# Scale and shift of the first layer by fp32 weights held in TensorE, with five row blocks of sixteen on VectorE

## The chip, the cores and the metric

The kernel is one program on one core of a Trainium2 chip. The metric is the device time of one execution in microseconds (us), the median over the runs. A profile of one execution lists every instruction of the engines: TensorE (PE for its matmuls, PEld for its loads of the stationary operand), VectorE (DVE), ScalarE (ACT), GpSimd (POOL) and SyncE (SP), on whose queue the loads from memory are issued.

## What is computed

Two layers of a backbone with four parallel branches work on 256 latent and 256 context tokens of 2048 features. The change is in the first step of the first layer, the adaptive normalisation (adaLN):

```python
shift, scale, gate = jnp.split(jax.nn.silu(c) @ w_ada[l] + b_ada[l], 3, axis=-1)
shift_c, scale_c, gate_c = jnp.split(jax.nn.silu(c_ctx) @ w_ada[l] + b_ada[l], 3, axis=-1)
h = modulate(x, g_pre[l], shift[:, None], scale[:, None])      # rms_norm(x, g) * (1 + scale) + shift
hc = modulate(ctx, g_pre[l], shift_c, scale_c)
p = split_proj(h @ w_in[l])
```

So two vectors, silu(c) for the latents (stream 0) and silu(c_ctx) for the context (stream 1), are multiplied by a matrix of 2048 rows; 4096 of its columns, shift and scale, are needed before the first projection can take its input. The normalisation needs the sum of squares of each token over the 2048 features. All is fp32.

## The kernel before

Features lie on the partitions, tokens along the free dimension: `x[k]`, k = 0 to 15, is 128 features by 512 tokens (both streams). A matmul of the projections splits each operand into a rounded part (`h`, made by ScalarE's cast) and the rest (`l`, made by VectorE's subtraction), both of type fp32r, and adds three products (`mm3`, L165 to L167 in the profile): hh x wh, hl x wh, hh x wl.

`startup` makes shift and scale in eight groups. Group g covers features of `x[2g]` and `x[2g+1]`: 512 columns, pieces of 128 for scale and shift of the two tiles. A group's weights are 2048 rows, that is 16 row blocks (`rb`) of 128 rows by 512 columns. They come in four units (q = 0 to 3) of 1 MB; a unit has two halves, a half two row blocks (the index i). The loads are issued in the order of the units, three buffers (`NRAW`) ahead. For each block ScalarE casts (L279) and VectorE subtracts (L286), and TensorE holds four columns of `sc4` (the two parts of the two vectors) and streams the block through, once for each part (L439, L440):

```python
w = self.sc4[:, 4 * rb:4 * rb + 4]
T.matmul(pa[g][0:4, :], w, hi[i], start=rb == 0, stop=False)
T.matmul(pa[g][0:4, :], w, lo[i], start=False, stop=rb == 15)
```

The result is four rows in the PSUM bank `pa`. ScalarE copies them (L446), four transposes bring them onto partitions (L451), VectorE adds the parts (L459, L461) and makes the factors `ab` (L410, L412), multiplies the two tiles of x by the tokens' reciprocal roots R (L454), and `build` modulates (ScalarE, L416) and splits them into `hh` and `hl` (L159, L160).

Between the groups the first seven column tiles of the projection are added up in seven banks (`pk`): for each k there are two units `wk`, of four and of three column tiles, so 12 and 9 matmuls. In groups 1 to 7 one such unit follows q = 1 and three follow q = 3: 42 `pk` matmuls a group. All engines take their instructions in the order in which the program writes them; `later(d, fn)` writes a piece d steps later, `defer` at the next half step.

Ahead of it `setup` loads x (16 loads of 256 KB), squares it (L370), adds the 16 squares on VectorE (L372), sums over the partitions with four small fp32 matmuls (`tok_sums`, L190, which holds 128x128 squares and streams two columns of ones), makes the reciprocal root (`rstd`, L176 to L182) and spreads it over the partitions by four transposes (`tok_bcast`, L196; R is its copy, L391).

After `startup` come the other projections, the branches, the second layer; VectorE makes the remaining adaLN columns there by multiply-and-add of loaded blocks (`ada_task`, L1098 and L1100).

Of the kernel before, what the change touches and what calls it, by code (L numbers as in the profile page):

```python
# [10 lines left out]
F32 = mybir.dt.float32  # L11
# [19 lines left out]
# column tiles of w_in, in the order in which the kernel consumes them  # L31
# [21 lines left out]
# columns of the table of per-feature parameters of a layer  # L53
# [9 lines left out]
class Step:  # L63
    __slots__ = ("unit", "half", "mm", "post", "pre", "pulls", "again", "cap")

    def __init__(self, unit, half, mm, post=None, pre=None, pulls=("", ""), again=False, cap=1.9):
        # again: the weights of this step are those that an earlier step of the unit has left
        # cap: the work that VectorE can take on in a pull, in us
        self.unit, self.half, self.mm, self.post, self.pre = unit, half, mm, post, pre
        self.pulls, self.again, self.cap = pulls, again, cap  # L70


class Unit:
    def __init__(self, src, widths, raw="raw", split="w", keep=False):
        # raw, split: where the loaded tile and its parts live; "u" is the common pool of 2 KB tiles
        # keep: a later step uses the parts again
        self.src, self.widths, self.keep = src, widths, keep
        self.rpool, self.spool = raw, split
        self.raw = None
        self.hi = {}  # L80
        self.lo = {}


class Kernel:
    NU = 73
    NRAW = 3
    NHI, NLO, LOOK = 4, 3, 3
    SLOW = 12
    KEPT = 14
    EARLY = (6, 14)  # L90

# [20 lines left out]
    # ---- allocation  # L112
# [25 lines left out]
    # ---- small helpers  # L138
    def defer(self, fn):
        # emitted at the next quarter of a unit, so that an engine need not wait for what precedes it  # L140
        self.dq.append(fn)
# [6 lines left out]
    def spend(self, w):  # L148
        # one more operation of VectorE on w columns: is that enough for this pull?
# [7 lines left out]
    def split(self, hi, lo, src, lag=False):  # L157
        # src = hi + lo exactly; both parts pass TensorE in one go each
# [26 lines left out]
    def tok_sums(self, acc, T, out):  # L185
        # out[:, 2j:2j+2] = the sum over partitions of token tile j, tokens on partitions
# [6 lines left out]
    def tok_bcast(self, r, T, out, step=2):  # L193
        # out[p, t] = r[t] for every partition p
# [4 lines left out]
    # ---- main program  # L199
# [8 lines left out]
    def pull(self, q):  # L208
        # the next piece of the first task; where that was a light one, one of the task behind it too
# [23 lines left out]
    def raw_dma(self, i):  # L233
        x = self.units[i]
        n = sum(x.widths)
        x.raw = self.u("raw") if x.rpool == "u" else self.rp.tile([128, 2048], F32, name=self.nm("raw"), tag="raw")
        self.nc.sync.dma_start(x.raw[:, 0:n], x.src)

    def run(self):
# [3 lines left out]
        nd, nh, nl, busy = 3, 0, 0, 3  # L243
        post = []

        def dmas():
            nonlocal nd, busy
            while nd < len(self.units) and (self.units[nd].rpool == "u" or busy < self.NRAW):
                busy += self.units[nd].rpool != "u"
# [3 lines left out]
        def ahead(i, n):  # L253
            # may the split of step i be issued now? n: buffers of the pool of the weight parts
            # at the start, where the loads hold the time, what is split early would keep other work waiting
# [4 lines left out]
            # a kept tile is in use up to its last step  # L260
# [14 lines left out]
        def hi_op(i):  # L275
            x, h = prog[i].unit, prog[i].half
            if prog[i].again:
                return
            x.hi[h] = piece(i, self.hp, "wh", lambda d, r, k: self.S.copy(d, r))  # L279

        def lo_op(i):
            nonlocal busy
            x, h = prog[i].unit, prog[i].half
            if prog[i].again:
                return
            x.lo[h] = piece(i, self.lp, "wl", lambda d, r, k: self.V.tensor_tensor(  # L286
                d, r, x.hi[h][k].bitcast(F32), ALU.subtract))
            left[id(x)] -= 1
            if not left[id(x)]:
                busy -= x.rpool != "u"  # L290
# [3 lines left out]
        for self.j, st in enumerate(prog):  # L294
# [22 lines left out]
            for part in range(2):  # L317
# [4 lines left out]
                st.mm(hi, lo, part)  # L322
            if st.post:
# [7 lines left out]
    # ---- set-up  # L331
    def setup(self):
# [13 lines left out]
        self.sc4 = self.const("sc4", 64, F32R)  # L346
# [7 lines left out]
        for i, n in enumerate(("ident", "cst", "perm")):  # L354
            nc.sync.dma_start(self.cs if n == "cst" else getattr(self, n), a[n])
            self.raw_dma(i)
        hsum = self.u("heads")
        nc.sync.dma_start(hsum[:, 0:96], a["hsum"])
        V.memset(self.ones, 1.0)
        th = self.sm(32)  # L360
# [3 lines left out]
        s4 = self.sc4.rearrange("p (n h) -> p n h", h=2)  # L364
        V.tensor_copy(s4[:, :, 0], self.sc)
        V.tensor_tensor(s4[:, :, 1], self.sc, s4[:, :, 0].bitcast(F32), ALU.subtract)
        sq = None
        for k in range(NK):
            t = self.u("sq")
            S.activation(t, self.x[k], AF.Square)  # L370
            if k:
                V.tensor_tensor(sq, sq, t, ALU.add)  # L372
            else:
                sq = t
        st = {}

        def sums():
            p = st["p"] = self.ps()
            self.tok_sums(sq, 512, p)

        def rstd():
            V.tensor_copy(self.sx, st["p"][:, 0:8])
            st["r"] = self.rstd(self.sx, 8, 1.0 / D)

        def bcast():
            p = st["p"] = self.ps()
            self.tok_bcast(st["r"], 512, p)

        def copy():
            self.R = self.u("R")  # L390
            S.copy(self.R, st.pop("p"))  # L391
        self.j = 0
        for i, fn in zip((0, 2, 4, 5), (sums, rstd, bcast, copy)):
            self.later(i, fn)
# [12 lines left out]
    # ---- the modulated, normalised input  # L407
# [10 lines left out]
    def startup(self):  # L418
        # scale and shift of layer 0 on TensorE, the first columns of its projection beside them
# [11 lines left out]
        pa = {}  # L431

        def ada(g, q, half):
            def mm(hi, lo, i):
# [3 lines left out]
                w = self.sc4[:, 4 * rb:4 * rb + 4]  # L438
                T.matmul(pa[g][0:4, :], w, hi[i], start=rb == 0, stop=False)  # L439
                T.matmul(pa[g][0:4, :], w, lo[i], start=False, stop=rb == 15)  # L440
            return mm

        def ada_post(g):
            def post():
                row = self.u("row")
                S.copy(row[0:4, :], pa.pop(g)[0:4, :])  # L446

                def cols():
                    pc = self.ps()
                    for j in range(4):  # L450
                        T.matmul(pc[:, 4 * j:4 * j + 4], row[0:4, j * 128:(j + 1) * 128], self.ident[0:4, 0:4],  # L451
                                 is_transpose=True)
                    for i in range(2):
                        V.tensor_tensor(self.x[2 * g + i], self.x[2 * g + i], self.R, ALU.mult)  # L454

                    def mods():
                        # stream 0: columns 0 and 1 of each tile, stream 1: columns 2 and 3
                        t = self.sm(16)
                        V.tensor_copy(t, pc[:, 0:16])  # L459
                        t4 = t.rearrange("p (j s h) -> p j s h", s=2, h=2)  # L460
                        V.tensor_tensor(t4[:, :, :, 0], t4[:, :, :, 0], t4[:, :, :, 1], ALU.add)  # L461
                        for i in range(2):
                            self.mod_cols(0, 2 * g + i, t4[:, 2 * i, :, 0], t4[:, 2 * i + 1, :, 0])
                    self.defer(mods)
                self.later(1, cols)
                for i in range(2):
                    self.later(2 + i, lambda i=i: build(2 * g + i))
# [18 lines left out]
        def add_ada(g, q):  # L486
            x = Unit(self.a["ada0"][4 * g + q], [1024, 1024], split="u")
# [12 lines left out]
        for g in range(8):  # L500
            # between the last of a group and the first of the next, the bank of the sums serves for their columns
# [7 lines left out]
    # ---- projections  # L509
    def store(self, l, n, i, p):  # L510
        # p: PSUM tile of projection column tile i of part n
# [49 lines left out]
    def proj_mm(self, box, xh, xl, T, half, nk=8):  # L561
        # box: list to hold the PSUM tile; contraction tiles half*nk .. of the moving operand's pieces
# [18 lines left out]
    # ---- pooling branch  # L581
# [65 lines left out]
    # ---- convolution branch  # L647
# [84 lines left out]
    def conv_pw(self, l):  # L732
        # the pointwise product of the convolution branch, as a unit of the main stream
# [29 lines left out]
    # ---- attention  # L763
    def attn(self, units):
        # one pull per stage; what a stage reads was made at least one pull earlier
# [35 lines left out]
    def att_s(self, x):  # L801
        # q: the two parts of a head one above the other, kd, kl: the first and the second part of its keys, each twice
# [13 lines left out]
    def stack(self, src, w):  # L816
        # for each head of a pair, both parts of its 64 rows in one tile; the first part lies where the head lay
# [7 lines left out]
    def double(self, src):  # L825
        # for each head of a pair, the first part of its 64 rows twice, and the second part twice
# [12 lines left out]
    def vstack(self, p3, h):  # L839
        # values of a head, tokens on partitions: for each token tile the two parts side by side  # L840
# [25 lines left out]
    def att_tr(self, x, c):  # L866
        # key tiles 2c and 2c+1, both query tiles; ctx queries have only the keys of c = 1
# [81 lines left out]
    def attn_c(self, l):  # L949
# [7 lines left out]
        # tile 0: the keys of both groups, tiles 1 to 4: the queries; rows of ss: 8 query heads, then 2 groups  # L957
# [92 lines left out]
    # ---- adaLN columns on VectorE  # L1050
    def ada_task(self, kind):
# [11 lines left out]
        # sums over partitions as rows of one bank, a row for each group and stream  # L1063
# [71 lines left out]
    # ---- layers  # L1135
# [32 lines left out]
    def values(self, l, g):  # L1168
        # four contraction tiles of the values of branch a, tokens on the partitions of the result
# [16 lines left out]
        def post():  # L1186
            # for each head the two parts of its values side by side
# [502 lines left out]
```

## Time and profile before

| | |
|---|---|
| Median of 3 runs | 2715.37 us (2715.2 to 2715.86) |
| Profiled execution: first to last instruction (span) | 2712.6 us; its own time is not listed apart from it |
| Mean granted clock of TensorE over the span | 0.997 of full |
| TensorE matmul busy | 2668.9 us |
| VectorE, ScalarE busy | 1880.6 us, 1187.7 us |
| Loads, mean over the span | 155 GB/s |

Times within the profile count from the first instruction. "Idle before" of a row is how long the engine stood idle just before it, with the instruction that ended the wait. The granted clock is a share of TensorE's 2.4 GHz; 0.5 is the other level, 1.2 GHz. The clock has no record ahead of the first change that it made, and counts as 1.00 until then. Matmuls overlap, so the distance between the starts of two rows says more than the length of one.

### The profile page before, as it was taken

How to read it: one execution, taken by the hardware profiler on the slowest of the kernel's cores; microseconds unless marked ns; L12 is line 12 of the kernel's file. 1: busy time of each engine (PE TensorE's matmuls, PEld its weight loads, DVE VectorE, ACT ScalarE, POOL GpSimd, SP SyncE). 2: the span in 40 equal slices, each digit the busy share in tenths (PEclk: the TensorE clock that was granted, in tenths of full speed). 3: DMA queues.
4: the chain of work that ended last, by engine and by line, in shares of the span. 5: the costliest groups of instructions: out<-in, count | busy, mean ns of one | idle time of the engine just before them, and what ended most of it. 6: DMA issues, size and time to landing. Idle time of an engine off the chain costs nothing.

```text
span 2712.6 us, 38481 instructions
## 1 busy us (share of the span) xinstructions
PE 2668.9 (98%) x15468; PEld 2320.9 (86%) x15468; DVE 1880.6 (69%) x2908; ACT 1187.7 (44%) x1866; POOL 0.2 (0%) x4
## 2 busy tenths in 40 slices
PE   6999999999999999999999999999999999999997
PEld 3678888788888888888888888899999999999997
DVE  8873667886487654677787565686787876875554
ACT  7852664345422223222222233466235764664443
POOL 0000000000000000000000000000000000000000
PEclk9999999999999999999999999999999999999999
DMA  8842224442232223445455355565335545445553
GB/s 333 294 165 101 88 101 152 148 145 81 83 119 94 100 94 109 148 171 198 168 171 184 118 197 200 186 222 187 109 115 175 179 150 175 148 149 183 185 186 119
DMA packets 106307, 422.42 MB, mean 156 GB/s; under 512 B 11624, under 2 KB 22288, under 8 KB 70416
## 3 DMA queue, kind: packets, MB, share of 16 engines
q1 hardware_dynamic: 106128, 419.96, 44.5%
q8 instruction: 121, 1.98, 0.3%
q14 instruction: 58, 0.48, 0.0%
HBM read 417.82 MB, written 2.10 MB: 155 GB/s over the span
## 4 chain that ended last, share of the span: by engine, by line
PE 94%; DVE 3%; ACT 2%; DMA 1%; issue 1%; SPq 0%; DVEq 0%; ACTq 0%
PE pm L165 23%; PE pm L166 23%; PE pm L167 23%; PE pb L165 3%; PE pb L167 3%; PE pb L166 3%; PE pk L165 1%; PE pk L166 1%; PE pk L167 1%; PE pt L872 1%; PE pv L166 1%; PE pv L167 1%; PE pv L165 1%; PE pa L440 1%; PE pa L439 1%; PE o L890 1%
## 5 line engine op out<-in xcount | busy, mean ns | idle before, releaser
L286 DVE TENSOR_TENSOR wl<-raw,wh 128x1024 fp32r<-128x1024 f32 (+1 forms) x720 | 779.5, 1098 | 668.6 <-PE pm L167 456.8
L279 ACT CAST wh<-raw 128x1024 fp32r<-128x1024 f32 (+1 forms) x720 | 671.1, 951 | 1282.0 <-PE pm L166 812.8
L165 PE MATMUL pm<-hh,wh 128*128 128x512 f32 (+1 forms) x3248 | 1097.4, 338 | 0.5 <-DVE tl L160 0.4
L167 PE MATMUL pm<-hh,wl 128*128 128x512 f32 (+1 forms) x3248 | 1088.1, 335 | 0.0
L166 PE MATMUL pm<-hl,wh 128*128 128x512 f32 (+1 forms) x3248 | 1087.8, 335 | 0.0
L165 PEld LDWEIGHTS pm<-hh,wh 128*128 128x128 f32 x3248 | 616.6, 190 | 65.3 <-issue 2.2
L167 PEld LDWEIGHTS pm<-hh,wl 128*128 128x128 f32 x3248 | 616.4, 190 | 62.7
L166 PEld LDWEIGHTS pm<-hl,wh 128*128 128x128 f32 x3248 | 616.9, 190 | 60.8
L1100 DVE SCALAR_TENSOR_TENSOR aacc<-aw,sc,aacc 128x512 f32<-128x512 f32 x420 | 291.1, 744 | 1.9 <-DMA aw<-in_adaD_dram 0.8
L165 PE MATMUL pm<-yh,wh 128*128 128x256 f32 (+1 forms) x544 | 177.9, 327 | 0.0
L167 PE MATMUL pm<-yh,wl 128*128 128x256 f32 (+1 forms) x544 | 177.7, 327 | 0.0
L166 PE MATMUL pm<-yl,wh 128*128 128x256 f32 (+1 forms) x544 | 177.7, 327 | 0.0
L672 DVE SCALAR_TENSOR_TENSOR cacc<-du,hlf,cacc 128x482 f32<-128x482 f32 (+29 forms) x240 | 145.1, 605 | 5.9
L165 PEld LDWEIGHTS pm<-yh,wh 128*128 128x128 f32 x544 | 103.5, 190 | 9.1
L166 PEld LDWEIGHTS pm<-yl,wh 128*128 128x128 f32 x544 | 103.5, 190 | 8.8
L167 PEld LDWEIGHTS pm<-yh,wl 128*128 128x128 f32 x544 | 103.5, 190 | 8.7
L858 ACT ACTIVATE P<-s,sm 128x512 f32<-128x512 f32 (+1 forms) x96 | 59.2, 617 | 92.8 <-DVE sm L857 87.3
L165 PE MATMUL pk<-hh,wh 128*128 128x256 f32 (+1 forms) x240 | 81.5, 339 | 0.1
L167 PE MATMUL pk<-hh,wl 128*128 128x256 f32 (+1 forms) x240 | 80.4, 335 | 1.1 <-DVE wl L286 1.1
L166 PE MATMUL pk<-hl,wh 128*128 128x256 f32 (+1 forms) x240 | 80.6, 336 | 0.5 <-DVE hl L160 0.5
L1239 DVE SCALAR_TENSOR_TENSOR mt<-mt,pb 128x512 f32<-128x512 f32 (+1 forms) x128 | 70.5, 551 | 11.8 <-ACT mt L1236 8.8
L160 DVE TENSOR_TENSOR tl<-pt,th 128x512 fp32r<-128x512 f32 x80 | 54.8, 686 | 18.8 <-ACT th L159 18.5
(277 smaller groups left out, 2912.5 us busy)
## 6 DMA issues: line engine op xcount, KB each, us to landing
raw<-in_wm_dram SPq DMA_DIRECT2D x229, 1024.0 KB, 4.9
aw<-in_adaD_dram SPq DMA_DIRECT2D x256, 256.0 KB, 5.4
raw<-in_ada_dram SPq DMA_DIRECT2D x32, 1024.0 KB, 5.0
raw<-in_wb_dram SPq DMA_DIRECT2D x64, 512.0 KB, 3.6
raw<-in_wv_dram SPq DMA_DIRECT2D x8, 1024.0 KB, 4.9
raw<-in_wk_dram SPq DMA_DIRECT2D x8, 1024.0 KB, 5.1
xr<-in_xT_dram SPq DMA_DIRECT2D x24, 256.0 KB, 5.4
x<-in_xT_dram SPq DMA_DIRECT2D x16, 256.0 KB, 5.0
```

What stands on the lines that cost most here:

```text
L160: sub = lambda: self.V.tensor_tensor(lo, src, hi.bitcast(F32), ALU.subtract)
L165: mm(out, wh, xh, start=first, stop=False)
L166: mm(out, wh, xl, start=False, stop=False)
L167: mm(out, wl, xh, start=False, stop=last)
L279: x.hi[h] = piece(i, self.hp, "wh", lambda d, r, k: self.S.copy(d, r))
L286: x.lo[h] = piece(i, self.lp, "wl", lambda d, r, k: self.V.tensor_tensor(d, r, x.hi[h][k].bitcast(F32), ALU.subtract))
L439: T.matmul(pa[g][0:4, :], w, hi[i], start=rb == 0, stop=False)
L440: T.matmul(pa[g][0:4, :], w, lo[i], start=False, stop=rb == 15)
L672: V.scalar_tensor_tensor(a3[:, :, lo:hi], u3[:, :, lo + d:hi + d], hlf[:, c:c + 1], a3[:, :, lo:hi], ALU.mult, ALU.add)
L858: S.activation(P[t], ss[t], AF.Exp, scale=0.125, bias=st[:, 2 + t:3 + t], accum_out=st[:, 4 + t:5 + t])
L1100: V.scalar_tensor_tensor(accs[s], w, c, accs[s], ALU.mult, ALU.add)
L1239: V.scalar_tensor_tensor(t, t, 1.0, q, ALU.add, ALU.mult)
```

## The change

- The adaLN weights of the stage are no longer split. A unit comes as four tiles of 128x512 (four loads of 256 KB where one of 1 MB stood), up to five units ahead (`NF`).
- For a row block TensorE now holds 128x128 pieces of the fp32 weights and streams the two columns of `sc` (both vectors, unsplit) through each: four fp32 matmuls (L468) that write two columns of `pa`. The result lies on the partitions at once, so the row copy, the transposes and the addition of parts go.
- In groups 1 to 7 five of the 16 blocks (`SHARE`) go to VectorE, which multiplies them by a column of `sc` and adds them up in two accumulators, one for each stream (L463, L465). At the last block but one, eight fp32 matmuls with `e2` sum the accumulators over the partitions into `pa` (L473).
- The squares of x are no longer added on VectorE: each of the 16 tiles goes to four fp32 matmuls with the columns of ones (L395). The reciprocal roots and R are made at once, with x times R of tiles 0 to 11 right behind, of tiles 12 to 15 at step 8.

```diff
+            if x.rpool == "f":
+                x.hi[h] = x.raw[2 * h:2 * h + 2]
+                return
...
+            if st.unit.rpool == "f" and st.half:
+                full -= 1
+                dmas()
...
+        p = self.ps()
         for k in range(NK):
             t = self.u("sq")
             S.activation(t, self.x[k], AF.Square)
-            if k:
-                V.tensor_tensor(sq, sq, t, ALU.add)
-            else:
-                sq = t
...
+            for j in range(4):
+                self.T.matmul(p[:, 2 * j:2 * j + 2], t[:, j * 128:(j + 1) * 128], self.ones[:, 0:2],
+                              start=k + j == 0, stop=k == NK - 1 and j == 3)
...
                 rb = 4 * q + 2 * half + i
-                w = self.sc4[:, 4 * rb:4 * rb + 4]
-                T.matmul(pa[g][0:4, :], w, hi[i], start=rb == 0, stop=False)
-                T.matmul(pa[g][0:4, :], w, lo[i], start=False, stop=rb == 15)
+                p, w = pa[g], hi[i]
+                if g and (half, i) in self.SHARE[q]:
+                    new = g not in accs
+                    if new:
+                        accs[g] = [self.u("acc") for _ in range(2)]
+                    for s, t in enumerate(accs[g]):
+                        c = self.sc[:, 2 * rb + s:2 * rb + s + 1]
+                        if new:
+                            V.tensor_scalar(t, w, c, None, ALU.mult)
+                        else:
+                            V.scalar_tensor_tensor(t, w, c, t, ALU.mult, ALU.add)
+                else:
+                    for j in range(4):
+                        T.matmul(p[:, 2 * j:2 * j + 2], w[:, j * 128:(j + 1) * 128], self.sc[:, 2 * rb:2 * rb + 2],
+                                 start=rb + j == 0, stop=rb == 15 and j == 3)
+                if g and rb == 14:
+                    for s, t in enumerate(accs.pop(g)):
+                        for j in range(4):
+                            T.matmul(p[:, 2 * j:2 * j + 2], t[:, j * 128:(j + 1) * 128], self.e2[:, 2 * s:2 * s + 2],
+                                     start=False, stop=False)
```

TensorE before, from the first blocks of group 1 (`pa` is the group's bank, `wh` and `wl` the parts of the weights, `x4` four instructions in a row of this kind):

```order
L439 MATMUL pa_358<-wh_328,sc_92 4x512
L440 MATMUL pa_358<-wl_332,sc_92 4x512
L439 MATMUL pa_358<-wh_329,sc_92 4x512
L440 MATMUL pa_358<-wl_333,sc_92 4x512
L451 MATMUL p_371<-ident,row_356 128x4 x4
L439 MATMUL pa_358<-wh_340,sc_92 4x512
L440 MATMUL pa_358<-wl_344,sc_92 4x512
```

Two matmuls of 512 columns stand there for a block, 32 for a group, and the transposes of the group ahead.

TensorE now, group 1 from its first `wk` unit's last matmuls to its last block (`aw` is a loaded 128x512 tile, `acc` an accumulator):

```order
L170 MATMUL pk_503<-hh_441,wl_475 128x512
L468 MATMUL pa_426<-sc,aw_352 128x2 x4
L468 MATMUL pa_426<-sc,aw_354 128x2 x4
L468 MATMUL pa_426<-sc,aw_355 128x2 x4
L468 MATMUL pa_426<-sc,aw_384 128x2 x4
L468 MATMUL pa_426<-sc,aw_385 128x2 x4
L468 MATMUL pa_426<-sc,aw_386 128x2 x4
L473 MATMUL pa_426<-e_92,acc_435 128x2 x4
L473 MATMUL pa_426<-e_92,acc_436 128x2 x4
L468 MATMUL pa_426<-sc,aw_387 128x2 x4
L168 MATMUL pk_579<-hh_441,wh_513 128x512
```

Ahead of these stand four more rows of L468 and twelve `pk` matmuls, behind them thirty. So a group is 44 + 8 fp32 matmuls of two columns, in two runs of 16 and 36.

VectorE now, at the same place, from group 1's factors to the `wl` of its first `wk` unit:

```order
L427 TENSOR_SCALAR ab_87<-pa_301,cs 128x2
L463 TENSOR_SCALAR acc_435<-aw_319,sc 128x512
L463 TENSOR_SCALAR acc_436<-aw_319,sc 128x512
L163 TENSOR_TENSOR hl_442<-x_95,hh_441 128x512
L465 SCALAR_TENSOR_TENSOR acc_435<-aw_321,sc,acc_435 128x512
L465 SCALAR_TENSOR_TENSOR acc_436<-aw_321,sc,acc_436 128x512
L163 TENSOR_TENSOR hl_464<-x_97,hh_463 128x512
L465 SCALAR_TENSOR_TENSOR acc_435<-aw_327,sc,acc_435 128x512
L465 SCALAR_TENSOR_TENSOR acc_436<-aw_327,sc,acc_436 128x512
L304 TENSOR_TENSOR wl_475<-raw_334,wh_473 128x512
```

The 16 subtractions of a group are gone from this queue; ten operations on the two accumulators stand among the splits of x and of the `wk` tiles.

## Rows read from the trace of the kernel before

**Rows 1.** The page, parts 1 and 4: busy time; chain by engine.

```profile
PE 2668.9 (98%) x15468; PEld 2320.9 (86%) x15468; DVE 1880.6 (69%) x2908; ACT 1187.7 (44%) x1866; POOL 0.2 (0%) x4
...
PE 94%; DVE 3%; ACT 2%; DMA 1%; issue 1%; SPq 0%; DVEq 0%; ACTq 0%
```

**Rows 2.** Stretches: length, then busy us and count by engine, clock, DMA.

```profile
core 0: us, PE busy (x) PEld busy (x) DVE busy (x) ACT busy (x) POOL busy (x), PEclk, DMA share, GB/s
0.00:39.05 39.05, 18.10 (x64) 5.82 (x64) 30.73 (x69) 29.24 (x51) 0.20 (x4) 0.98 0.93 353
...
48.71:153.92 105.21, 105.21 (x470) 64.99 (x470) 91.44 (x179) 83.44 (x161) 0.00 (x0) 1.00 0.85 308
```

**Rows 3.** The chain that ended last, 0 to 175 us: start, length, what.

```profile
48.71 0.34 PE p L451 x4
...
153.92 0.34 PE p L451 x4
```

**Rows 4.** TensorE's matmuls in order of time, 17 to 24 us: start, length, what.

```profile
17.85 1.87 PE L190 MATMUL p<-ones,sq 128*128 128x2 f32 x8 [17.85 <-DVE sq L372]
19.58 0.59 PE L439 MATMUL pa<-wh,sc 128*4 128x512 f32 x1
19.96 0.63 PE L440 MATMUL pa<-wl,sc 128*4 128x512 f32 x1
...
23.38 0.56 PE L440 MATMUL pa<-wl,sc 128*4 128x512 f32 x1
23.77 0.40 PE L439 MATMUL pa<-wh,sc 128*4 128x512 f32 x1
```

**Rows 5.** The same from 30 to 49 us, and the stage's last `pa`.

```profile
35.05 0.39 PE L439 MATMUL pa<-wh,sc 128*4 128x512 f32 x1
37.67 0.59 PE L440 MATMUL pa<-wl,sc 128*4 128x512 f32 x1 [2.23 <-DVE wl L286]
...
40.50 0.53 PE L165 MATMUL pk<-hh,wh 128*128 128x512 f32 x1
40.86 0.39 PE L166 MATMUL pk<-hl,wh 128*128 128x512 f32 x1
...
151.47 0.40 PE L440 MATMUL pa<-wl,sc 128*4 128x512 f32 x1
```

**Rows 6.** TensorE's loads of the stationary operand, 1742.9 to 1744.6 us.

```profile
1743.06 0.54 PEld L190 LDWEIGHTS p<-ones,sq 128*128 128x128 f32 x4
1743.52 0.97 PEld L190 LDWEIGHTS p<-ones,xz 128*128 128x128 f32 x8
1744.41 0.19 PEld L165 LDWEIGHTS pm<-yh,wh 128*128 128x128 f32 x1
```

**Rows 7.** Stretches around the clock's fall, columns as in rows 2.

```profile
34.00:37.00 3.00, 1.39 (x5) 0.18 (x4) 2.93 (x11) 1.26 (x3) 0.00 (x0) 1.00 1.02 421
37.00:40.40 3.40, 2.73 (x6) 1.21 (x7) 2.51 (x5) 3.34 (x7) 0.00 (x0) 0.55 0.94 316
```

**Rows 8.** Groups by form: VectorE and ScalarE to 165 us; L1100, whole span.

```profile
L286 DVE TENSOR_TENSOR wl<-raw,wh 128x512 fp32r<-128x512 f32 x144 | 90.4, 684 | 7.8 <-ACT wh L279 4.6 <-issue 3.1
L279 ACT CAST wh<-raw 128x512 fp32r<-128x512 f32 x144 | 79.0, 616 | 6.5 <-DMA raw<-in_ada_dram 3.7 <-PE pk L166 2.8
L1100 DVE SCALAR_TENSOR_TENSOR aacc<-aw,sc,aacc 128x512 f32<-128x512 f32 x420 | 291.1, 744 | 1.9 <-DMA aw<-in_adaD_dram 0.8
```

**Rows 9.** All engines in order of time, from five places up to 40 us.

```profile
4.10 1.40 ACT L370 ACTIVATE sq<-x 128x512 f32<-128x512 f32 x2 [1.42 <-DMA x<-in_xT_dram]
...
23.68 0.16 DVE L382 COPY sx<-p 128x8 f32<-128x8 f32 x1
...
25.41 0.65 PE L196 MATMUL p<-ident,sm 128*128 128x128 f32 x4
...
36.28 0.29 DVE L410 TENSOR_SCALAR ab<-sm,cs 128x2 f32<-128x2 f32 x1
...
39.12 0.69 DVE L286 TENSOR_TENSOR wl<-raw,wh 128x512 fp32r<-128x512 f32 x1
```

More of the change, by code (lines that the diff above doesn't have):

```diff
@@ L87 @@
     NHI, NLO, LOOK = 4, 3, 3
+    NF = 5
     SLOW = 12
@@ L90 @@
     EARLY = (6, 14)
+    SHARE = (((0, 1), (1, 1)), ((0, 1), (1, 1)), ((0, 1),), ())
     def __init__(self, ctx, tc, a, out):
@@ L235, in raw_dma @@
         n = sum(x.widths)
+        if x.rpool == "f":
+            x.raw = [self.u("aw") for _ in range(4)]
+            for k, t in enumerate(x.raw):
+                self.nc.sync.dma_start(t, x.src[:, k * 512:k * 512 + 512])
+            return
         x.raw = self.u("raw") if x.rpool == "u" else self.rp.tile([128, 2048], F32, name=self.nm("raw"), tag="raw")
@@ L242, in run @@
         left = {id(x): len(x.widths) for x in self.units}
-        nd, nh, nl, busy = 3, 0, 0, 3
+        nd, nh, nl, busy, full = 4, 0, 0, 0, 4
         post = []
         def dmas():
-            nonlocal nd, busy
-            while nd < len(self.units) and (self.units[nd].rpool == "u" or busy < self.NRAW):
-                busy += self.units[nd].rpool != "u"
+            nonlocal nd, busy, full
+            while nd < len(self.units):
+                p = self.units[nd].rpool
+                if p == "raw" and busy == self.NRAW or p == "f" and full == self.NF:
+                    break
+                busy += p == "raw"
+                full += p == "f"
                 self.raw_dma(nd)
@@ L278, in hi_op @@
                 return
+            if x.rpool == "f":
+                x.hi[h] = x.raw[2 * h:2 * h + 2]
+                return
             x.hi[h] = piece(i, self.hp, "wh", lambda d, r, k: self.S.copy(d, r))
@@ L285, in lo_op @@
                 return
+            if x.rpool == "f":
+                x.lo[h] = None
+                return
             x.lo[h] = piece(i, self.lp, "wl", lambda d, r, k: self.V.tensor_tensor(
@@ L289, in lo_op @@
             if not left[id(x)]:
-                busy -= x.rpool != "u"
+                busy -= x.rpool == "raw"
                 dmas()
@@ L345, in setup @@
         self.sc = self.const("sc", 32)
-        self.sc4 = self.const("sc4", 64, F32R)
+        self.e2 = self.const("e2", 4)
         self.hlf = self.const("hlf", 2 * (4 * TAPS + 8))
@@ L354, in setup @@
         for i, n in enumerate(("ident", "cst", "perm")):
+            self.raw_dma(i)
             nc.sync.dma_start(self.cs if n == "cst" else getattr(self, n), a[n])
-            self.raw_dma(i)
         hsum = self.u("heads")
         nc.sync.dma_start(hsum[:, 0:96], a["hsum"])
+        self.raw_dma(3)
         V.memset(self.ones, 1.0)
+        V.memset(self.e2, 0.0)
+        for i in (0, 3):
+            V.memset(self.e2[:, i:i + 1], 1.0)
         th = self.sm(32)
@@ L363, in setup @@
         V.tensor_scalar(self.sc, self.sc, 0.5, None, ALU.mult)
[L364 to L367, printed above, removed]
+        p = self.ps()
         for k in range(NK):
@@ L370, in setup, with normal @@
             S.activation(t, self.x[k], AF.Square)
-            if k:
-                V.tensor_tensor(sq, sq, t, ALU.add)
-            else:
-                sq = t
[L375 to L391, printed above, removed]
+            for j in range(4):
+                self.T.matmul(p[:, 2 * j:2 * j + 2], t[:, j * 128:(j + 1) * 128], self.ones[:, 0:2],
+                              start=k + j == 0, stop=k == NK - 1 and j == 3)
+        V.tensor_copy(self.sx, p[:, 0:8])
+        r = self.rstd(self.sx, 8, 1.0 / D)
+        p = self.ps()
+        self.tok_bcast(r, 512, p)
+        R = self.u("R")
+        S.copy(R, p)
+        def normal(*ks):
+            for k in ks:
+                V.tensor_tensor(self.x[k], self.x[k], R, ALU.mult)
+        normal(*range(12))
         self.j = 0
-        for i, fn in zip((0, 2, 4, 5), (sums, rstd, bcast, copy)):
-            self.later(i, fn)
+        self.later(8, lambda: normal(12, 13, 14, 15))
         V.tensor_copy(self.onesr, self.ones)
@@ L429, in build @@
             self.x[k] = None
-        pa = {}
+        pa, accs = {}, {}
         def ada(g, q, half):
@@ L444, in post, with mods @@
             def post():
[L445 to L452, printed above, removed]
-                    for i in range(2):
[L454 to L465, printed above, removed]
+                p = pa.pop(g)
+                def mods():
+                    for i in range(2):
+                        self.mod_cols(0, 2 * g + i, p[:, 4 * i:4 * i + 2], p[:, 4 * i + 2:4 * i + 4])
+                self.defer(mods)
                 for i in range(2):
-                    self.later(2 + i, lambda i=i: build(2 * g + i))
+                    self.later(1 + i, lambda i=i: build(2 * g + i))
             return post
@@ L486, in add_ada @@
         def add_ada(g, q):
-            x = Unit(self.a["ada0"][4 * g + q], [1024, 1024], split="u")
+            x = Unit(self.a["ada0"][4 * g + q], [1024, 1024], raw="f", split="u")
             for half in range(2):
```

## The prediction

> **What bounds the kernel now.** I read the page first: TensorE is busy 98% of the span and has 94% of the chain that ended last [rows 1]. So the change pays or costs only where it alters what TensorE does or waits for. Then I cut the span at the stage that changes. Up to 39 us TensorE has 18.10 us of work; from 48.71 to 153.92 us it has no idle time, although VectorE is also busy for 91.44 of the 105.21 us [rows 2]. The chain shows the rhythm: the transposes that close a group (L451) return from 48.71 to 153.92 us in six equal steps [rows 3], 17.53 us each. Per step TensorE issues 32 `pa` and 42 `pk` matmuls of 512 columns at about 0.23 us, and four small transposes: 74 x 0.23 + 0.34 = 17.4 us. That is the whole step. VectorE (0.68 us for each subtraction, 16 per group for these weights) and ScalarE (0.62 us for each cast) [rows 8] work beside it and lengthen nothing there. Only ahead of group 1's first `pk` does VectorE hold TensorE up: nothing starts from 35.05 + 0.39 to 37.67 us [rows 5]. My mark is the end of the last `pa` matmul, 151.47 + 0.23 = 151.70 us [rows 5]. What follows it is listed in the same order before and after on TensorE but for the transposes, and is TensorE's, so a shift of this mark is a shift of the end.
>
> **What a new matmul costs.** The change makes the 128x128 fp32 weight block the stationary operand and streams two columns through it. The trace has this very form: `tok_sums` (L190) puts a 128x128 fp32 block under two columns of ones. Four such matmuls stand there as eight loads and eight matmuls [rows 4, 6]: two passes each. At full clock twelve passes lead from the load at 1743.06 us to the next stage's load at 1744.41 us [rows 6]: 0.1125 us a pass, 0.225 us a matmul. In the start the eight take 17.85 to 19.58 us [rows 4], 0.216 us a pass; the matmuls right behind are also slow (8 in 19.96 to 23.38 us, 0.43 us against 0.23 later [rows 4]). Pass and matmul both halve in rate together, so a pass costs 0.1125 us at 2.4 GHz and 0.216 us at 1.2 GHz.
>
> **The change part by part.** A block cost two 512-column matmuls, 0.46 us. It now costs four fp32 matmuls, 8 passes: 0.90 us at the full clock, 1.73 us at half. Five of 16 blocks leave TensorE in groups 1 to 7, but the two accumulators come back as eight matmuls, 16 passes; so 11 x 8 + 16 = 104 passes replace 32 matmuls and the transposes. The new product needs 11.7 us a group at full clock where 7.7 us stood. The squares' sums add 16 x 4 matmuls, 128 passes, where 8 were, ahead of everything else on TensorE's queue. VectorE loses 10.9 us a group (16 x 0.684), ScalarE 9.9 us, and VectorE gets ten operations of at most 0.744 us (L1100 is the nearest row [rows 8]): 7.4 us. With the 4.3 us a step left from rows 2 once its subtractions are taken off, it has under 12 us a step: cheap, and hidden under TensorE's 21 us or more. The loads become four of 256 KB each; a group and its `wk` tiles are 5.1 MB, 12.1 us at the 421 GB/s seen at 34 to 37 us [rows 7], hidden too. On SP's queue the extra issues stand only ahead of loads of the same stage.
>
> **The clock.** It decides the size. The trace has two rises and one fall in this stage. TensorE worked from 17.85 us, and its matmuls still went at 0.43 us until about 23.4: passes first, then 3.8 us of 512-column matmuls [rows 4]. The second time it worked from 37.67 us, with wide matmuls alone, and was fast again from 40.86 us, after about 3 us [rows 5]. The fall: the last matmul started at 35.05 us, the granted clock was still 1.00 to 37.00 us and 0.55 over 37.0 to 40.4 [rows 5, 7]. So the passes seem not to have helped the first rise, and the fall came some two microseconds after the last wide matmul ended. No row here has a long run of passes, so the trace does not settle what they do. The Trainium skill, TensorE: Matmul & The Clock Gate, section What's actually happening, says that a monitor sets the clock by how busy the engine has been recently; passes that stand back to back would keep it at 2.4 GHz. The same page, section Part 4: PE-mode transpose, says that transposes do not count as busy in the same way, so not all work does. By the first the sum would be the rival's +32 us, by the second the forecast's +112 us. From the slow first rise in the rows alone I take half clock in long runs of passes.
>
> **The sum, half clock.** The first square is done at 4.8 us [rows 9]. 128 passes x 0.216 = 27.6 us, to 32.4. The way from the sums to the broadcast's end was 23.68 to 26.06 us [rows 9], 2.4 us; with a semaphore, 35.0. Group 0: 128 passes, to 62.6. Its scale, shift and first split take VectorE and ScalarE some 7 us, beside group 1's first 32 passes (6.9 us). Then 12 `pk` matmuls, 8 at 0.43 us while the clock rises and 4 at 0.23: 4.4 us. Then 72 passes, 18 of them (2 us, as at the fall) still fast: 2.0 + 54 x 0.216 = 13.7 us. Group 1 ends at 87.6 us. A step from there: 30 `pk` matmuls, 8 slow, 8.5 us; 32 passes, 18 fast, 5.0 us; 12 matmuls 4.4 us; 72 passes 13.7 us; together 31.6. If the clock falls only after 32 passes, the first run of passes stays fast and so do the 12 matmuls: 8.5 + 3.6 + 2.8 + 12.2 = 27.1 us. I take the middle, 29.3 us, an estimate. Six steps: 87.6 + 175.8 = 263.4 us against 151.7, **+111.7 us**. On the profiled span of 2712.6 us that is 2824.3; the median of the runs is 2.8 us above that span, so 2827 us. With 27.1 us a step it is 2814; with every pass at 0.216 us (a step of 35.4 us) 2866. What the change takes away, the stall at 35.4 us among it, is in the comparison of the marks.
>
> **Rivals.** *Passes keep the clock up.* For: nothing idles between them. Against: the slow first rise. Sums to 20.9 us (rising clock included), broadcast 23.5, group 0 at 37.9. Group 1: 3.6 us of passes; a wait of about 3 us, since `wl` of the first `wk` tile stands on VectorE's queue behind two `hl` and six accumulations (in the trace from L410 at 36.28 to that L286's end at 39.81 us is 3.5 us with one `hl` and none of them [rows 9]), and `pk` waits for it; 2.8 + 8.1 us. That gives 55.4; six steps of 11.7 + 9.7 = 21.4 us lead to 183.8: +32 us, 2747 us. *A long run of passes is cheaper than L190's short ones*, so that TensorE is relieved with the other two engines. For: the twelve are few and stand between other work. Against: they are equally spaced at either clock. Were it half the price, 0.1125 us a matmul, a step would be 15.5 us; group 1 would end near 44 us, held by x times R on VectorE (16 x 0.68 us ahead of the first scale) and the chain above; 44 + 93 = 137 us, 15 us earlier, 2701 us. It decides from 0.154 us a matmul downwards: 40 + 36c + 6 x (9.7 + 52c) = 151.7. *TensorE is not the limit but VectorE's accumulations*, for which the four matmuls per accumulator wait: their ten operations come to 7.4 us in a step of 21 us or more and their weights are up to five units ahead, so this adds at most the last operation, under 1 us a step, on either clock.
>
> **How the numbers follow.** Half clock 58%, full clock 30%, cheap passes 7%, something between or behind 5%. The likeliest gives 2827 us, by itself 2805 to 2866. Range 2738 to 2862: nearly all of the first, most of the second. Runs of this kernel agree within 0.03%, and 0.2% (5.4 us) is what a measurement can tell. Faster 7%, same 3%, slower 90%.
>
> **What would show it.** Right: L395 and L468 passes spaced 0.216 us up to about 62 us, a granted clock near 0.5 there and between 0.5 and 0.9 in later steps, `pa` ending near 263 us, VectorE at half load in the stage, the rest of the span unchanged. Full clock: spacing 0.11 us, steps of 21.4 us, the mark near 184. Wrong altogether: passes under 0.08 us, steps under 17.5 us, idle TensorE waiting for loads or VectorE.

## The result and the profile after

The changed kernel takes 2834.12 us, the median of 4 runs (2830.94 to 2835.91); the kernel before took 2715.28 us beside it (4 runs, 2715.13 to 2715.86). The ratio is 1.0434, with a 95% interval of 1.0421 to 1.0447: slower by 118.8 us. The profiled span is 2830.8 us, so it grew by 118.2 us, and TensorE's mean granted clock fell from 0.997 to 0.974.

The page of the changed kernel, the parts that answer to [rows 1]:

```profile
PE 2801.8 (99%) x16156; PEld 2491.0 (88%) x16156; DVE 1834.4 (65%) x2820; ACT 1118.1 (39%) x1730; POOL 0.2 (0%) x4
...
PE 96%; DVE 2%; ACT 1%; issue 0%; DMA 0%; SPq 0%; DVEq 0%; ACTq 0%
```

TensorE is busy for 132.9 us more than before, VectorE for 46.2 and ScalarE for 69.6 us less. The engines that were relieved are not the ones the end waits for.

Stretches of the changed kernel, columns as in [rows 2]:

```profile
core 0: us, PE busy (x) PEld busy (x) DVE busy (x) ACT busy (x) POOL busy (x), PEclk, DMA share, GB/s
40.00:62.00 22.00, 22.00 (x105) 22.00 (x105) 6.29 (x18) 0.00 (x0) 0.00 (x0) 1.00 0.81 298
...
90.00:200.00 110.00, 110.00 (x525) 98.83 (x525) 40.30 (x75) 18.44 (x35) 0.00 (x0) 0.68 0.48 148
```

In both TensorE never idles. From 90 to 200 us its clock is granted at 0.68 on average, where [rows 2] had 1.00 from 48.71 to 153.92 us; VectorE works 40.30 us of 110, and the DMA engines are busy for 0.48 of the stretch. The 1.00 of the first stretch says nothing: the first clock change on record comes later, at 74.6 us. There the count tells the clock: 105 passes in 22.00 us are 0.21 us each.

TensorE's matmuls of the changed kernel in order of time, up to 118 us (start, length, what; `x` counts passes):

```profile
4.69 27.46 PE L395 MATMUL p<-ones,sq 128*128 128x2 f32 x128 [4.69 <-ACT sq L393]
33.91 1.12 PE L199 MATMUL p<-ident,sm 128*128 128x128 f32 x4 [1.76 <-DVE sm L185]
34.82 34.13 PE L468 MATMUL pa<-sc,aw 128*128 128x2 f32 x160
...
73.66 0.63 PE L170 MATMUL pk<-hh,wl 128*128 128x512 f32 x1
74.08 7.12 PE L468 MATMUL pa<-sc,aw 128*128 128x2 f32 x48
81.06 3.55 PE L473 MATMUL pa<-e,acc 128*128 128x2 f32 x16
84.48 1.84 PE L468 MATMUL pa<-sc,aw 128*128 128x2 f32 x8
...
91.45 0.51 PE L168 MATMUL pk<-hh,wh 128*128 128x512 f32 x1
91.80 0.40 PE L169 MATMUL pk<-hl,wh 128*128 128x512 f32 x1
...
95.67 4.23 PE L468 MATMUL pa<-sc,aw 128*128 128x2 f32 x32
...
105.03 7.12 PE L468 MATMUL pa<-sc,aw 128*128 128x2 f32 x48
112.02 3.55 PE L473 MATMUL pa<-e,acc 128*128 128x2 f32 x16
115.43 1.84 PE L468 MATMUL pa<-sc,aw 128*128 128x2 f32 x8
```

The 128 passes of the sums take 27.46 us, the 160 of group 0 and of group 1's first run 34.13 us: 0.214 and 0.213 us a pass, the rate of the eight in [rows 4]. The `pk` matmuls between 69.4 and 74.08 us stand 0.43 us apart like those at 19.96 to 23.38 us in [rows 4]. Only then, at 74.6 us, does the clock rise, and most of the passes that follow are fast: 48 would take 10.2 us at 0.213 and 5.4 us at 0.1125, and they take 7.12, so about 31 of them are fast. Then it falls, and the last 24 take 3.55 and 1.84 us, 0.22 us each. The second group repeats this: its `pk` matmuls turn fast between 91.45 and 91.80 us, about 5.4 us after they began; its passes end at 115.43 + 1.84 = 117.27 us, 30.95 us behind group 1's (86.32).

From the same view at 246 to 272 us, the first run of passes of the last group and the stage's last `pa` row, which answers to the last of [rows 5]:

```profile
249.99 3.63 PE L468 MATMUL pa<-sc,aw 128*128 128x2 f32 x32
...
267.47 1.85 PE L468 MATMUL pa<-sc,aw 128*128 128x2 f32 x8
```

The mark stands at 269.3 us instead of 151.7: 117.6 us later, of 118.2 us of the whole span. What follows the stage costs what it did, within 0.6 us.

The waits of the changed kernel, 0 to 290 us (engine, what, line, for what; us in total, times, longest):

```profile
DVE ab L425 <- PE pa L468: 97.5, 8, 15.9
```

VectorE spends 97.5 us of the stage waiting for TensorE's `pa`. Before, at group 1, TensorE waited for VectorE [rows 5].

### The profile page after: what moved, and what is told of

It is laid out like the page before. It is cut to its first block, busy times and chain, and to the rows that moved or that the text cites. A ratio compares the mean times of both kernels' runs of the same rounds, so it can differ in the third digit from the quotient of the medians.

```text
span 2830.8 us, 39798 instructions
## 1 busy us (share of the span) xinstructions
PE 2801.8 (99%) x16156; PEld 2491.0 (88%) x16156; DVE 1834.4 (65%) x2820; ACT 1118.1 (39%) x1730; POOL 0.2 (0%) x4
## 4 chain that ended last, share of the span: by engine, by line
PE 96%; DVE 2%; ACT 1%; issue 0%; DMA 0%; SPq 0%; DVEq 0%; ACTq 0%
PE pm L168 22%; PE pm L169 22%; PE pm L170 22%; PE pa L468 4%; PE pb L168 3%; PE pb L169 3%; PE pb L170 3%; PE pk L168 2%; PE pk L169 2%; PE pk L170 2%; PE pt L891 1%; PE pv L168 1%; PE pv L170 1%; PE pv L169 1%; PE p L395 1%; PE pa L473 1%
## 5 line engine op out<-in xcount | busy, mean ns | idle before, releaser
L304 DVE TENSOR_TENSOR wl<-raw,wh 128x1024 fp32r<-128x1024 f32 (+1 forms) x592 | 701.9, 1188 | 700.1 <-PE pm L170 457.6
L294 ACT CAST wh<-raw 128x1024 fp32r<-128x1024 f32 (+1 forms) x592 | 603.7, 1023 | 1319.3 <-PE pm L169 812.6
L468 PEld LDWEIGHTS pa<-sc,aw 128*128 128x128 f32 x744 | 126.2, 266 | 1.5
L468 PE MATMUL pa<-sc,aw 128*128 128x2 f32 x744 | 124.3, 303 | 0.0
L168 PE MATMUL pk<-hh,wh 128*128 128x256 f32 (+1 forms) x240 | 94.0, 392 | 0.0
L169 PE MATMUL pk<-hl,wh 128*128 128x256 f32 (+1 forms) x240 | 91.4, 381 | 0.3 <-DVE hl L163 0.3
L170 PE MATMUL pk<-hh,wl 128*128 128x256 f32 (+1 forms) x240 | 90.5, 377 | 1.1 <-DVE wl L304 1.1
```

The lines of the kernel that those rows point to most:

```text
L168: mm(out, wh, xh, start=first, stop=False)
L169: mm(out, wh, xl, start=False, stop=False)
L170: mm(out, wl, xh, start=False, stop=last)
L468: T.matmul(p[:, 2 * j:2 * j + 2], w[:, j * 128:(j + 1) * 128], self.sc[:, 2 * rb:2 * rb + 2], start=rb + j == 0, stop=rb == 15 and j == 3)
```

## The experiments

Theory: in long runs of two-column passes the clock falls to 1.2 GHz, and most of the loss is that; the rest is that a block costs more passes' time than its two wide matmuls did. Rival: the passes are dear for another reason (the fp32 loads themselves, the data's arrival, VectorE's accumulators), and the clock is an effect beside it.

**All fp32 matmuls 128 columns wide.** The same loads and blocks; the two columns are read 64 times, so that each pass streams 128 columns. The matmuls of the accumulators and of the squares are widened likewise (the squares' with 128 columns of ones), and VectorE reads the results from the first two columns of each 128. No other work changes. The edit at the weights:

```diff
-                        T.matmul(p[:, 2 * j:2 * j + 2], w[:, j * 128:(j + 1) * 128], self.sc[:, 2 * rb:2 * rb + 2],
+                        T.matmul(p[:, 128 * j:128 * j + 128].rearrange("p (r c) -> p r c", c=2), w[:, j * 128:(j + 1) * 128],
+                                 self.sc[:, 2 * rb:2 * rb + 2].unsqueeze(1).to_broadcast([128, 64, 2]),
...
```

> Every fp32 matmul of the stage (of the weights, of the accumulators, of the squares) streams 128 columns, the two columns 64 times over, instead of 2; weights loaded, number of passes and order are those of the change. Clock theory (the long runs of two-column passes let the clock fall to half, and that is most of the loss): the clock stays at or near full, passes come 0.11 us apart, steps fall from 30.7 to about 21.4 us, and the loss is the 32 us of the full-clock sum: 2747 us, 2742 to 2765. Rival (a pass costs 0.21 us in a long run whatever is streamed, because of its loads of fp32 weights, the transfers or VectorE beside it): no gain, 2834 us or more, with passes still 0.21 us apart.

Measured: 2743.93 us, ratio to before 1.0104 (1.0087 to 1.0121), as the clock theory had it. Its matmuls in order of time:

```profile
5.41 15.98 PE L395 MATMUL p<-ones,sq 128*128 128x128 f32 x128 [5.41 <-ACT sq L393]
...
23.63 18.03 PE L469 MATMUL pa<-sc,aw 128*128 128x128 f32 x160
...
42.52 0.50 PE L168 MATMUL pk<-hh,wh 128*128 128x512 f32 x1 [0.86 <-ACT wh L294]
...
44.94 0.50 PE L170 MATMUL pk<-hh,wl 128*128 128x512 f32 x1 [1.68 <-DVE wl L304]
...
63.82 3.73 PE L469 MATMUL pa<-sc,aw 128*128 128x128 f32 x32
...
85.04 3.73 PE L469 MATMUL pa<-sc,aw 128*128 128x128 f32 x32
```

Its stretches:

```profile
42.00:50.00 8.00, 5.80 (x22) 4.61 (x23) 7.16 (x12) 2.01 (x4) 0.00 (x0) 0.79 0.99 330
50.00:180.00 130.00, 130.00 (x902) 119.62 (x902) 62.57 (x120) 32.42 (x61) 0.00 (x0) 1.00 0.71 248
```

The same 160 loads take 18.03 us where they took 34.13, and the clock is 1.00 from 50 to 180 us. With the loads, blocks and accumulators unchanged, the rival falls. Of 118.8 us, 2834.1 - 2743.9 = 90.2 us come back with the clock. The other 28.2 us (2743.93 against 2715.71 of before in these runs) are dearer work, with 2.5 us of waits at 42 to 45 us and a short fall of the clock behind them.

**64 columns**, the same edit with 32 repetitions.

> The same with 64 columns instead of 128. Clock theory: somewhere between the two, depending on whether this half-way load keeps the clock; nearest row is the fall of before, where four 512-column matmuls in 3 us did not keep it, so rather near 2834 (2790 to 2834) than near 2747. Rival: 2834.

Measured: 2770.58 us, ratio 1.0202 (1.0182 to 1.0223). The expectation failed: it had 2790 to 2834, nearer to the changed kernel than to that of 128 columns. Its matmuls:

```profile
4.46 27.57 PE L395 MATMUL p<-ones,sq 128*128 128x64 f32 x128 [4.46 <-ACT sq L393]
...
34.69 34.23 PE L469 MATMUL pa<-sc,aw 128*128 128x64 f32 x160
...
72.64 0.39 PE L168 MATMUL pk<-hh,wh 128*128 128x512 f32 x1
...
88.22 3.68 PE L469 MATMUL pa<-sc,aw 128*128 128x64 f32 x32
```

Here the sums and group 0 ran as slowly as with two columns, and yet from the tenth `pk` matmul on (72.64 us) the stage was fast: 32 passes took 3.68 us against 4.23. So the clock's part of the loss comes apart in two. This kernel's rows stand 88.22 - 63.82 = 24.4 us behind those of 128 columns, and its span is longer by as much (2768.4 against 2744.0 us): that is the start. From there to the changed kernel's span of 2830.8 us it is 62.4 us: that is the alternation of the clock in groups 1 to 7.

**128 columns for the sums, 64 for the weights.** If it is the state reached in the start that decides, the kernel of 64 columns should be at the full clock throughout once the sums have raised the clock.

```diff
-                self.T.matmul(p[:, 2 * j:2 * j + 2], t[:, j * 128:(j + 1) * 128], self.ones[:, 0:2],
+                self.T.matmul(p[:, 128 * j:128 * j + 128], t[:, j * 128:(j + 1) * 128], self.ones[:, 0:128],
...
```

> The 64-column variant, but with 128 columns in the sums of squares alone, which raised the clock at 8.4 us in the 128-column variant. If 64 columns keep a clock that has risen and only fail to raise it, the whole stage runs at full clock: 2744 us (2740 to 2750), as with 128. If they let it fall: 2770 us or more.

Measured: 2746.28 us, ratio 1.0115 (1.0094 to 1.0135), within the range expected. Its matmuls:

```profile
4.60 16.80 PE L395 MATMUL p<-ones,sq 128*128 128x128 f32 x128 [4.60 <-ACT sq L393]
...
23.64 17.98 PE L469 MATMUL pa<-sc,aw 128*128 128x64 f32 x160
```

The same 160 passes of 64 columns take 17.98 us behind sums of 16.80 us and 34.23 us behind sums of 27.57 us. What a pass costs here hangs on what ran before it. Between 42 and 50 us, where TensorE waits as in the kernel of 128 columns, the granted clock was 0.59 here and 0.79 there.

**The sums of squares back on VectorE**, the rest of the change kept.

```diff
...
-            for j in range(4):
-                self.T.matmul(p[:, 2 * j:2 * j + 2], t[:, j * 128:(j + 1) * 128], self.ones[:, 0:2],
-                              start=k + j == 0, stop=k == NK - 1 and j == 3)
+            if k:
+                V.tensor_tensor(sq, sq, t, ALU.add)
+            else:
+                sq = t
+        self.tok_sums(sq, 512, p)
```

> The change without its sums of squares on TensorE: VectorE adds the 16 squares as before, and four small matmuls sum them. Clock theory: the sums end near 19.7 us instead of 32.2, all behind them moves by 12.5 us, and with steps that repeat at the clock's rhythm by 9 to 15: 2821 us (2818 to 2825). Rival (the sums were hidden by the loads of the first group): within 3 us of 2834.

Measured: 2818.09 us, ratio 1.038 (1.0364 to 1.0396), 16.0 us under the change, at the lower end of the range expected; its four runs lie between 2815.03 and 2824.54 us. Its matmuls:

```profile
18.46 1.87 PE L193 MATMUL p<-ones,sq 128*128 128x2 f32 x8 [18.46 <-DVE sq L396]
...
22.98 34.13 PE L471 MATMUL pa<-sc,aw 128*128 128x2 f32 x160
```

Group 0 starts 11.8 us earlier and is as slow. The sums are a small part of the loss, about 16 of 118.8 us.

**The sums of squares on TensorE alone**, in the kernel before.

> The kernel before with this part of the change alone: the sums of squares on TensorE, all else as before. The 128 passes end near 32.2 us at half clock; group 0, which then has its parts ready, takes 9 us and group 1's wait on VectorE shrinks: 7 us slower than before, 2722 us (2719 to 2727). If passes ran at full clock the sums would end near 20 us and there would be no change.

Measured: 2725.09 us, ratio 1.0034 (1.002 to 1.0047): 9.4 us slower than before, within the range expected. Its matmuls:

```profile
4.66 27.46 PE L373 MATMUL p<-ones,sq 128*128 128x2 f32 x128 [4.66 <-ACT sq L371]
...
48.65 0.50 PE L165 MATMUL pk<-hh,wh 128*128 128x512 f32 x1 [0.39 <-ACT wh L279]
```

The sums end at 32.1 us instead of 19.6, and the first `pk` matmul comes at 48.65 instead of about 39.1. So this part alone costs time, less than the 12.5 us by which the sums end later.

**No block on VectorE, and ten blocks.** Five blocks a group were moved; none and ten price a block.

```diff
-    SHARE = (((0, 1), (1, 1)), ((0, 1), (1, 1)), ((0, 1),), ())
+    SHARE = ((), (), (), ())
```

In the second, this line stands there:

```diff
+    SHARE = (((0, 1), (1, 0), (1, 1)), ((0, 1), (1, 0), (1, 1)), ((0, 0), (0, 1), (1, 1)), ((0, 1),))
```

> The change with no row block on VectorE: all 16 go to TensorE in every group and the eight matmuls of the accumulators go. 128 passes a group instead of 104. Clock theory with 0.216 us for each pass added to the long runs: 24 x 0.216 = 5.2 us a group, 36 us in all, 2870 us (2855 to 2890, since the steps repeat at the clock's rhythm). Rival (part of the loss is that the accumulations on VectorE make TensorE or the loads wait): less than 36 us more, or a gain.

Measured: 2862.89 us, ratio 1.0544 (1.0523 to 1.0565), 28.8 us over the change. Seven groups have 5 x 8 - 16 = 24 passes more each: 168, at 0.171 us, between the two levels. The time lies in the range of the clock theory, but less than 36 us more was also named as the rival's sign, so the time alone does not tell them apart. A stretch of it does, beside that of the changed kernel at 90 to 200 us:

```profile
90.00:200.00 110.00, 110.00 (x525) 100.72 (x525) 14.95 (x35) 19.05 (x36) 0.00 (x0) 0.66 0.45 140
```

TensorE is busy for 110.00 of 110.00 us with the accumulations and without them, so they make it wait for nothing there.

> The change with 10 of 16 blocks on VectorE instead of 5: 64 passes a group, in runs of 16 and 48, and 20 operations on VectorE, 14.9 us, so 19 us a step there. Clock theory: 40 passes fewer give 7 x 8.6 = 60 us back if all ran at half, more if the shorter runs keep the clock, down to VectorE's 19 us a step: 2750 to 2785 us. Rival (VectorE is the limit of the change): slower than 2834.

Measured: 2788.33 us, ratio 1.027 (1.0249 to 1.029), 45.8 us under the change; just outside the range expected. A stretch of it:

```profile
90.00:200.00 110.00, 97.58 (x510) 87.60 (x508) 80.16 (x140) 22.74 (x42) 0.00 (x0) 0.80 0.64 211
```

and two of its matmuls:

```profile
101.21 2.90 PE L473 MATMUL pa<-e,acc 128*128 128x2 f32 x16 [1.69 <-DVE acc L465]
...
124.20 3.57 PE L473 MATMUL pa<-e,acc 128*128 128x2 f32 x16 [2.86 <-DVE acc L465]
```

With ten blocks TensorE idles 12.4 of 110 us, in five waits that are all for the accumulators. With five it idled 0.00. So the prediction's third rival exists, at a share which the change does not have.

**128 columns, nine blocks on VectorE, and the sums back there**, in search of a version that beats both kernels. It has the edits of the first and of the fourth experiment, with the sums, the roots and x times R spread over later steps as before; a group's product is then 7 x 8 + 16 = 72 passes, 8.0 us at full clock, near the 7.7 us of before.

```diff
-    SHARE = (((0, 1), (1, 1)), ((0, 1), (1, 1)), ((0, 1),), ())
+    SHARE = (((0, 1), (1, 0), (1, 1)), ((0, 1), (1, 0), (1, 1)), ((0, 1), (1, 1)), ((0, 1),))
...
+                if g < 6:
+                    self.later(4, lambda: self.normal(2 * g + 4, 2 * g + 5))
```

> Towards a version that beats both: 128 columns streamed as in the wide variant, nine of 16 blocks on VectorE, sums of squares on VectorE with their steps spread as before, x times R in pairs with the groups. A step has 72 passes at 0.11 us and 42 matmuls at 0.23: 17.7 us, as VectorE's 9 x 1.49 + 4.3 = 17.7. Clock theory: a step like that of before (17.53 us), first group about as early: 2716 us (2710 to 2724). It cannot be clearly faster than before as long as TensorE and VectorE share the work alone.

Measured: 2750.31 us, ratio 1.0127 (1.011 to 1.0144). The expectation failed. TensorE's waits, 0 to 190 us:

```profile
PE pa L487 <- DVE acc L478: 17.9, 7, 3.3
```

VectorE's waits in the same stretch:

```profile
DVE ab L438 <- PE pa L481: 24.6, 7, 4.5
```

Each engine waits for the other seven times. On VectorE's queue the factors `ab` (77.34 us), which wait for the group's `pa`, stand ahead of the next group's accumulations (81.82 to 96.2 us), and TensorE waits for those from 92.26 to 95.57 us. In its stretch from 90 to 120 us TensorE is busy for 23.53 of 30.00 us and the clock is at 0.90. So relief of TensorE by moving blocks ended in a loop of waits here. How much of the 34 us over the forecast is the loop and how much the clock was not separated, and another order of VectorE's queue was not tried.

**VectorE's subtractions to GpSimd**, in the kernel before: one in four of L286 in the units of groups 0 and 1, and then three in eight. It asks whether a lighter VectorE alone helps the start, where TensorE waited for it [rows 5].

```diff
-            x.lo[h] = piece(i, self.lp, "wl", lambda d, r, k: self.V.tensor_tensor(
+            early = x.rpool == "raw" and self.units.index(x) < 9 and x.spool == "u"
+            x.lo[h] = piece(i, self.lp, "wl", lambda d, r, k: (self.G if early and (k and h) else self.V).tensor_tensor(
...
```

> Not the change, but the kernel before, with one in four of the subtractions L286 of its first units (groups 0 and 1) on GpSimd, which is idle. It tests the reading of the start: TensorE waits for VectorE there up to 40 us, and its work up to the last pa of group 1 (18 us from 19.6) would end near 38 to 41 us instead of 46.5. If VectorE sets the start, 2 to 6 us faster: 2709 to 2713 us. If the loads set it, no change; if GpSimd is slow or holds VectorE up at a shared port, slower.

> The same with three in eight of the subtractions on GpSimd. If VectorE sets the start and GpSimd keeps up, as fast or 1 to 2 us faster than with a quarter (2708 to 2712 us); if GpSimd becomes the late one, slower than with a quarter.

Measured: 2720.11 us (ratio 1.0015, 1.0005 to 1.0024) and 2721.86 us (1.0022, 1.0013 to 1.0031). Both missed the gains of up to 8 us that they had if VectorE sets the start, and came out 4.2 and 6.0 us slower than before. The group of GpSimd in the first of the two, 0 to 60 us, then that of VectorE's products x times R in it, 0 to 50 us, and the same group in the kernel before:

```profile
L287 POOL TENSOR_TENSOR wl<-raw,wh 128x512 fp32r<-128x512 f32 x8 | 14.8, 1854 | 36.3 <-ACT wh L279 35.7 <-PE pa L441 0.6
```

```profile
L455 DVE TENSOR_TENSOR x<-x,R 128x512 f32<-128x512 f32 x2 | 2.4, 1224 | 0.0
```

```profile
L454 DVE TENSOR_TENSOR x<-x,R 128x512 f32<-128x512 f32 x2 | 1.3, 682 | 0.0
```

A subtraction takes 1.85 us on GpSimd on average, and VectorE's product of x and R takes 1224 ns beside it instead of 682. TensorE also waited 2.8 us for GpSimd's `wl`. VectorE was not relieved as meant, so whether a lighter VectorE would shorten the start stays open.

## Why the prediction was right

**The bound.** TensorE was to remain the bound, with VectorE's and ScalarE's relief worth nothing: from 90 to 200 us it is busy for 110.00 of 110.00 us, and VectorE waits for it for 97.5 us of the stage.

**The price of a pass.** 0.1125 us at the full clock and 0.216 at half were taken from twelve and eight passes. Measured: 0.113 us in the kernel of 128 columns (18.03 us for 160, at the full clock) and 0.213 in the changed kernel. A matmul of two passes at full clock, 0.225 us, stays above the 0.154 us from which "cheap passes" would have decided.

**The clock.** That long runs of passes go at half clock was a choice on thin rows, with 58%; the rows did not settle it, and so far it was luck that it came true. The kernel of 128 columns shows the clock as the cause of most of the loss: 90.2 of 118.8 us. The Trainium skill, TensorE: Matmul & The Clock Gate, section What's actually happening, has the clock follow how busy the engine has been. This case's trace does not agree with what the prediction drew from it, that passes back to back would stay at 2.4 GHz: TensorE and its loads were busy for 22.00 of 22.00 us at 40 to 62 us, at 0.21 us a pass.

**The first part of the sum.** Sums to 32.4 us, measured 32.15; broadcast to 35.0, measured 34.8; group 0 to 62.6, where VectorE's first factors came at 62.2 us. Group 1 to 87.6, measured 86.3: its 12 `pk` matmuls took 5.1 us, all of them slow, instead of 4.4, and its 72 passes 12.2 us instead of 13.7.

**The step: the term that was mis-sized.** 29.3 us was the middle of 27.1 and 31.6; measured are (269.3 - 86.3) / 6 = 30.5 us, nearer the upper end: five steps of 31.0 us and a last one of 28.1, the only one in which the clock stayed up through the run of 32 passes (3.63 us at 249.99), as the lower case has it. Six steps of 1.2 us more make 7.2 us, less 1.3 of group 1: the mark came 5.9 us later than forecast and the time 7.1 us. For five of the six steps the upper case had the right course, the clock down in either run of passes, and two sizes in it were off in opposite directions: it counted too few slow `pk` matmuls and too few fast passes. Step by step, from 86.3 to 117.3 us:

| part of a step | upper case | measured | why |
|---|---|---|---|
| 30 `pk` matmuls | 8.5 us | 9.4 us | about 12 slow instead of 8 |
| 32 passes | 5.0 us | 4.2 us | about 26 fast instead of 18 |
| 12 `pk` matmuls | 4.4 us | 5.1 us | all slow instead of 8 |
| 72 passes | 13.7 us | 12.2 us | about 31 fast instead of 18 |

The counts solve 0.43 n + 0.23 (30 - n) = 9.4 for slow `pk` matmuls and 0.213 (32 - n) + 0.1125 n = 4.2, with 72 and 12.2 in its place, for fast passes. The rise came some 5.4 us after the `pk` matmuls began where the 3 us of [rows 5] had been carried over, and the fall came later, too. So that the forecast lies within 7.1 us of the measured time is in part these errors offsetting each other.

**The rival "passes keep the clock up"** was priced at 2747 us, with steps of 21.4 us, the mark at 183.8 and a wait of 3 us ahead of group 1's `pk` matmuls. The kernel of 128 columns is that case: 2743.9 us, 85.04 - 63.82 = 21.2 us, and 0.86 + 1.68 = 2.5 us of waits. So the change loses 28 us even when the clock holds: 104 passes at 0.11 us cannot replace 32 matmuls at 0.23 us.

**The rival "VectorE's accumulations limit"** did not happen with five blocks (TensorE idled 0.00 of 110 us); it does with ten (12.4 us).

What stays open is why the 64-column passes stayed slow behind the slow sums and fast behind the fast ones; the runs show that they did, not what in them decided.

## What to carry to other kernels

Before a vector-matrix product is turned so that the matrix becomes the stationary operand, multiply the loads of the stationary operand by the time of one, and look up in the trace what the clock did during a long run of such loads: where the rows are few and slow, price the whole run at the slow level. If it must be done so, try to stream the small operand repeatedly: here 128 columns instead of two cost nothing a pass and gave back 90 of 119 us. Relieving engines that waited for the bound was worth nothing, and moving more work onto a queue that itself waited for the bound made a loop of waits.

## What was not expected of the hardware

- Streaming 128 columns instead of two through a 128x128 fp32 block made a pass no longer: 160 took 18.03 us, 0.113 us each, and 32 behind `pk` matmuls 3.73 us.
- The same 160 passes of 64 columns went in 34.23 us in one kernel and in 17.98 us in another, by what ran ahead of them.
- With subtractions on GpSimd (1854 ns each on average), an operation on VectorE beside them took 1224 instead of 682 ns on average.
